# Four-layer diffusion block on one core: the first gate and up tiles of each layer by eight plain block products instead of seven-product sums

## The chip, the core and the metric

The kernel runs on one core of a Trainium2 chip. The metric is the device time of one execution in microseconds (us). TensorE (PE in the rows) multiplies, VectorE (DVE) and ScalarE (ACT) prepare operands and evacuate results, GpSimd (POOL) helps, and SyncE (SP) issues nearly all loads from one in-order queue.

## The reference

Each of four layers is a token mixer (four different ones) followed by a SwiGLU feed-forward block. Only the second half matters here:

```
xs = xs + ms[2] * os_                                   # mixer's residual, through w_o
h  = modulate(rms_norm(xs, norm2_g[li]), ms[3], ms[4])
xs = xs + ms[5] * ((silu(h @ w_gate) * (h @ w_up)) @ w_down)
```

There are 1024 features, 2816 hidden features and 640 tokens (512 latent, 128 context), and each layer also needs its modulation vectors, `silu(cond) @ w_mod`, a 1024 by 6144 matrix.

## The kernel before, in words

Values are split into a rounded high part and a remainder (`hi`, `lo`), and every product is three matmuls: hi·hi, hi·lo, lo·hi. Activations lie features by tokens. The 2816 hidden features are 22 tiles of 128; tile i and tile i + 11 form pair i, and each pair has a gate matrix and an up matrix (`mats`, m = 0 to 21: gate of pair 0, up of pair 0, gate of pair 1, and so on).

For one such matrix the weights A are two by two blocks (tile i or i + 11, by the two halves of 512 features) and the activations B are two by two blocks (feature half, by token halves of 320). `gate_up` takes the four result blocks from seven block products in place of eight: 11·11, 12·21, S2·T2, S1·T1, S3·T3, 22·T4 and S4·22. S1 to S4 are sums of weight blocks that DVE makes (`make_a`), T1 to T4 are sums of activation blocks (`make_b`). A block product is four feature slices of three matmuls, 128x128 weights by 320 tokens. Each weight block or sum is split by a cast on ACT (`whi`) and a subtraction on DVE (`wlo`) in `two`. `Net.slot` hands out the buffers in turn: 4 for loaded blocks (`raw`), 9 each for `whi` and `wlo`, 4 for sums.

The order around the change, in `rest`: the last two output tiles of the w_o projection are computed token half by token half (`halves_first`), so that the RMS norm of the first half (`stat`: squares, a sum over partitions by PE, `rstd`) can go on while PE works on the second half. `make_b` is a generator: its first eight steps make blocks 11 and 21 (first token half), its ninth, in the program of before, makes T1 to T4 and block 22. The generators of the first two matrices are advanced between these steps. `fill` issues pieces of the next layer's modulation product: a burst of 16 small matmuls (32 in the trace) over four 512 KB loads (`rawm`, four buffers), whose buffers can be loaded again only when PE has read them. A scheduler then sets the final order on each engine, so the program's text gives only priorities. In layer 4 there is no next layer and no burst.

`self.sq`, `raws`, `rstd` and the names `hh`/`hl` are the squares, the scaled inputs, the norm's factors and the high and low parts of activation blocks; `big` and `sm` are PSUM tiles, `t` the squares' tile and `x` the residual stream.

Of the kernel before, what the change touches and what calls it, by code (L numbers as in the profile page):

```python
# [8 lines left out]
F32 = mybir.dt.float32  # L9
F32R = mybir.dt.float32r  # L10
# [4 lines left out]
P = 128  # L15
# [4 lines left out]
T = 640  # L20
# [242 lines left out]
class Net:  # L263
# [361 lines left out]
    def make_b(self, pool, L, B, raws):  # L625

        nc = self.nc
        lo, hi = slice(0, 320), slice(320, T)  # L630
        t3 = [pool.tile([P, 2, 320], F32, tag="a", name="raw", bufs=16) for _ in range(HALF // 2)]
        slots = [self.new_act() for _ in range(ND)]
        for tag, w in (("c", T), ("d", 320)):
            slots += [[pool.tile([P, w], F32R, tag=x + tag, name=x, bufs=HALF) for x in ("hh", "hl")] for _ in range(HALF)]
        shift = self.mods[L][0][:, 24:24 + ND]
        more = pool.tile([P, ND + HALF], F32, tag="more", name="more")
        self.sub(nc.vector, more[:, :ND], shift[:, :, 1], shift[:, :, 0])
        self.sub(nc.vector, more[:, ND:], shift[:, HALF:, 0], shift[:, :HALF, 0])

        done = []  # L640

        def two(name, slot, c, x, bias=None):
            h, l = (y[:, c] for y in slots[slot])
            if bias is None:
                nc.scalar.copy(h, x)  # L645
                done.append(self.sub(nc.vector, l, x, h.bitcast(F32)))
            else:
                nc.scalar.activation(h, x, AF.Identity, bias=bias)
                done.append(nc.vector.scalar_tensor_tensor(l, x, bias, h.bitcast(F32), ALU.add, ALU.subtract))  # L649
            B.setdefault(name, []).append((h, l))  # L650

        def raw(d, c):
            with contextlib.ExitStack() as st:
                if len(done) >= 2:
                    st.enter_context(self.tc.issue_after(done[-2].ins))
                nc.vector.tensor_tensor(raws[d][:, c], raws[d][:, c], self.rstd[:, c], ALU.mult)

        for d in range(ND):
            raw(d, lo)
            two(("11", "21")[d // HALF], d, lo, raws[d][:, lo], shift[:, d, 0:1])  # L660
            yield
        for i in range(HALF):
            for d in (i, i + HALF):
                raw(d, hi)
                p, m = raws[d][:, NL:], more[:, d:d + 1]
                nc.scalar.activation(p, p, AF.Identity, bias=m)
            a, b, t = raws[i], raws[i + HALF], t3[i // 2][:, i % 2]
            self.sub(nc.vector, t, b[:, hi], a[:, hi])
            self.sub(nc.vector, a[:, hi], a[:, hi], a[:, lo])
            two("T1", i, hi, a[:, hi])  # L670
        for i in range(HALF):
            a, b, t = raws[i], raws[i + HALF], t3[i // 2][:, i % 2]
            nc.vector.tensor_tensor(a[:, lo], t, a[:, lo], ALU.add)
            two("T2", ND + i, lo, a[:, lo], shift[:, i + HALF, 0:1])
            self.sub(nc.vector, b[:, lo], b[:, lo], a[:, lo])
        for i in range(HALF):
            two("T3", ND + i, hi, t3[i // 2][:, i % 2], more[:, ND + i:ND + i + 1])
        for i in range(HALF):
            two("T4", ND + HALF + i, lo, raws[i + HALF][:, lo])
        for i in range(HALF):  # L680
            two("22", i + HALF, hi, raws[i + HALF][:, hi], shift[:, i + HALF, 0:1])
        yield

    def make_a(self, L, name, i):
# [13 lines left out]
    def block(self, out, A, B, start, stop):  # L698

        h, l = self.two(A, self.nc.vector)  # L700
        for k, (xh, xl) in enumerate(B):
            c = slice(k * P, (k + 1) * P)
            self.mm(out, h[:, c], xh, start and k == 0, False)
            self.mm(out, h[:, c], xl, False, False)
            self.mm(out, l[:, c], xh, False, stop and k == len(B) - 1)

    def gate_up(self, fp, L, name, i, B, pair):

# [28 lines left out]
        self.block(a, A["12"], B["21"], False, True)  # L737
        result(0, 0, a)
        yield
        if i == 0:  # L740
            self.block(d, A["S1"], B["T1"], True, True)
        self.block(b, A["S2"], B["T2"], True, True)
        add(v1, b, s1)
        if i:
            self.block(d, A["S1"], B["T1"], True, True)
        self.block(b, A["S3"], B["T3"], False, True)
        yield
        add(v2, b, s1)
# [3 lines left out]
        self.block(d, A["S4"], B["22"], False, True)  # L752
        result(0, 1, d, v1)
        if up:
            for r in (1, 0):
                hi, lo = (fp.tile([P, T], F32R, tag="a", name=n, bufs=16) for n in ("ah", "al"))
                nc.scalar.copy(hi, pair[r])
                self.sub(nc.vector, lo, pair[r], hi.bitcast(F32))
                pair[r] = (hi, lo)
        yield  # L760


# [36 lines left out]
    def rest(self, L):  # L799

        nc, tc, a = self.nc, self.tc, self.a
        with tc.tile_pool(name=f"ffn{L}", bufs=1, reuse_waits="tile") as fp:
# [24 lines left out]
            def ahead(m):  # L827
                n, i = mats[m]
                gens[m] = self.gate_up(fp, L, n, i, B, pairs[i])
                next(gens[m])  # L830
            ahead(0)
            ahead(1)
            next(gens[0])
            next(gens[1])
            next(B_steps)
            for part, (i0, i1) in enumerate(PAIRS):
                if part:
                    ahead(2 * i0)
                for m in range(2 * i0, 2 * i1):
                    if m > 1:  # L840
                        next(gens[m])
                    next(gens[m])
                    if 0 < m < 2 * i1 - 1:
                        ahead(m + 1)
                    next(gens[m])
                    while done < todo * (m + 1) // len(mats):
                        self.fill(1)
                        done += 1
# [906 lines left out]
```

## Time and profile before

| | us |
|---|---|
| median of 3 runs (lowest, highest) | 3220.17 (3213.5, 3220.33) |
| the profiled execution, its own time | 3216.05 |
| its span in the trace | 3214.0 |
| PE busy with matmuls | 3029.7 (94%) |
| DVE busy | 2161.6 (67%) |
| ACT busy | 1528.5 (48%) |
| mean granted TensorE clock | 0.976 |

The span runs from the first to the last instruction in the trace; the execution's own time has 2.05 us around it. A busy PE is an upper bound, since matmuls overlap. The mean clock says that a small part of the span ran at the lower of TensorE's two levels, 1.2 and 2.4 GHz.

### The profile page before, as it was taken

To read this page: it belongs to the slowest core of one execution; us is meant where nothing else is said; L and a number is where in the kernel's file an instruction comes from. 1 tells how busy PE (TensorE), PEld (TensorE's weight loads), DVE (VectorE), ACT (ScalarE), POOL (GpSimd) and SP (SyncE) were. 2 spreads that over 40 slices of the span, in tenths; PEclk is the share of its full clock that TensorE was granted. 3 is DMA by queue.
4 is the path that set the end of the run, shared out by engine and by line. 5 is a ranking of instruction groups with operands and counts; after the bars stand their busy time and mean duration, and the time that the engine had idled before them with its cause. 6 is when DMAs were issued, how large, how long until landed. Compare 5 with 4: busy or idle time off the path is not lost.

```text
span 3214.0 us, 57273 instructions
## 1 busy us (share of the span) xinstructions
PE 3029.7 (94%) x21901; PEld 2841.6 (88%) x21901; DVE 2161.6 (67%) x4522; ACT 1528.5 (48%) x3264; POOL 607.1 (19%) x691
## 2 busy tenths in 40 slices
PE   7998989999999989999986899899999999899999
PEld 6997879999988779999985778899998878799999
DVE  5555587666586768585768766867575775875765
ACT  4555454333356755242446664434243576543432
POOL 2553200000044420000025542000001553100000
PEclk9998999999999999999998999999999999899999
DMA  8346563232433342222211224522233111132322
GB/s 265 97 123 208 176 224 102 70 92 94 147 102 128 112 155 76 83 83 76 87 53 37 63 75 143 170 89 80 83 132 118 52 32 32 53 99 70 96 66 86
DMA packets 159027, 331.41 MB, mean 103 GB/s; under 512 B 18592, under 2 KB 40480, under 8 KB 158752
## 3 DMA queue, kind: packets, MB, share of 16 engines
q1 hardware_dynamic: 155584, 323.46, 32.3%
q8 instruction: 173, 2.83, 0.4%
q10 hardware_dynamic: 3168, 4.28, 0.4%
q14 instruction: 102, 0.84, 0.1%
HBM read 303.86 MB, written 4.28 MB: 96 GB/s over the span
## 4 chain that ended last, share of the span: by engine, by line
PE 81%; DVE 8%; DMA 5%; ACT 3%; issue 1%; POOL 1%; SPq 0%; DVEq 0%; ACTq 0%; POOLq 0%
PE big L271 53%; PE sm L271 18%; PE S L271 6%; PE tp L1009 3%; DMA rawm<-in_wmod 3%; DMA k<-k 1%; PE tp L271 1%; DMA raw<-in_wall 1%; DVE st L1030 1%; ACT p L1031 1%; DVE x L603 1%; DVE wlo L319 1%; ACT pt L285 0%; DVE qs L958 0%; DVE hl L999 0%
## 5 line engine op out<-in xcount | busy, mean ns | idle before, releaser
L271 PE MATMUL big<-hh,whi 128*128 128x320 f32 x2720 | 825.4, 313 | 11.7 <-ACT hh L645 5.6
L271 PE MATMUL big<-hl,whi 128*128 128x320 f32 x2720 | 829.0, 311 | 6.3 <-DVE hl L649 3.6
L271 PE MATMUL big<-hh,wlo 128*128 128x320 f32 x2720 | 821.0, 310 | 0.0
L318 ACT CAST whi<-raw 128x512 fp32r<-128x512 f32 (+2 forms) x636 | 383.3, 607 | 709.2 <-PE big L271 554.0
L271 PEld LDWEIGHTS big<-hh,whi 128*128 128x128 f32 x2720 | 508.8, 190 | 25.8 <-ACT hh L645 7.8
L271 PEld LDWEIGHTS big<-hl,whi 128*128 128x128 f32 x2720 | 510.1, 189 | 12.0 <-DVE hl L649 6.2
L271 PEld LDWEIGHTS big<-hh,wlo 128*128 128x128 f32 x2720 | 508.2, 189 | 0.1
L319 POOL TENSOR_TENSOR wlo<-raw,whi 128x512 fp32r<-128x512 f32 (+2 forms) x148 | 196.7, 1342 | 1634.0 <-ACT whi L318 1600.6
L319 DVE TENSOR_TENSOR wlo<-raw,whi 128x512 fp32r<-128x512 f32 (+1 forms) x488 | 325.1, 670 | 142.1 <-ACT whi L318 136.1
L318 ACT CAST whi<-sum 128x512 fp32r<-128x512 f32 x352 | 217.6, 619 | 300.1 <-PE big L271 264.6
L271 PE MATMUL big<-ah,wlo 128*128 128x320 f32 x1408 | 329.1, 309 | 0.0
L271 PE MATMUL big<-ah,whi 128*128 128x320 f32 x1408 | 329.0, 310 | 0.0
L271 PE MATMUL big<-al,whi 128*128 128x320 f32 x1408 | 328.6, 309 | 0.0
L319 DVE TENSOR_TENSOR wlo<-sum,whi 128x512 fp32r<-128x512 f32 x352 | 240.8, 684 | 54.5 <-ACT whi L318 52.9
L1041 POOL TENSOR_SCALAR p<-p,st 128x640 f32<-128x640 f32 (+2 forms) x256 | 197.7, 778 | 285.2 <-DVE st L1040 172.0
L603 DVE SCALAR_TENSOR_TENSOR x<-big,mod,x 128x128 f32<-128x128 f32 (+2 forms) x384 | 146.2, 432 | 150.7 <-PE big L271 150.3
L271 PEld LDWEIGHTS big<-ah,whi 128*128 128x128 f32 x1408 | 237.3, 188 | 1.3 <-issue 0.8
L271 PEld LDWEIGHTS big<-al,whi 128*128 128x128 f32 x1408 | 237.3, 188 | 0.3
L271 PEld LDWEIGHTS big<-ah,wlo 128*128 128x128 f32 x1408 | 237.3, 188 | 0.2
L271 PE MATMUL sm<-whi,hh 128*128 128x256 f32 (+1 forms) x770 | 225.1, 297 | 1.7 <-DVE qs L287 1.1
L271 PE MATMUL sm<-wlo,hh 128*128 128x256 f32 (+1 forms) x770 | 223.3, 292 | 0.2 <-POOL wlo L319 0.2
L271 PE MATMUL sm<-whi,hl 128*128 128x256 f32 (+1 forms) x770 | 223.1, 291 | 0.0
(260 smaller groups left out, 5419.3 us busy)
## 6 DMA issues: line engine op xcount, KB each, us to landing
raw<-in_wall SPq DMA_DIRECT2D x676, 256.0 KB, 2.6
rawm<-in_wmod SPq DMA_DIRECT2D x176, 512.0 KB, 5.8
k<-k SPq DMA_DIRECT2D x38, 384.0 KB, 4.2
bias<-in_nabias SPq DMA_DIRECT2D x16, 576.0 KB, 7.2
raw<-in_wmod SPq DMA_DIRECT2D x32, 256.0 KB, 5.7
qpe<-pes SPq DMA_DIRECT2D x56, 80.0 KB, 2.1
raw<-in_wall SPq DMA_DIRECT2D x32, 128.0 KB, 2.1
out_y<-x ACTq DMA_DIRECT2D x8, 320.0 KB, 2.2
```

The costliest lines, as they stand in the source:

```text
L271: return self.nc.tensor.matmul(out, lhsT=lhsT, rhs=rhs, start=start, stop=stop, skip_group_check=True)
L318: self.nc.scalar.copy(hi, raw)
L319: eng.tensor_tensor(lo, raw, hi.bitcast(F32), ALU.subtract)
L603: self.last = self.nc.vector.scalar_tensor_tensor(xs, halves[b][:, p0:p1], self.mcol(L, i, d, c), xs, ALU.mult, ALU.add)
L1009: self.nc.tensor.transpose(out, in_, self.net.ident)
L1030: nc.vector.tensor_reduce(nm, s, axis=AX.XY, op=ALU.max, negate=True)
L1031: nc.scalar.activation(p.rearrange("p (a b) -> p a b", a=2), s, AF.Exp, bias=nm, accum_out=den)
L1041: nc.gpsimd.tensor_scalar(p, p, rd, 1.0, ALU.mult, ALU.mult)
```

## The change

For pair 0 of each layer a new generator `first_pair` replaces the two seven-product generators. It loads the four weight blocks of gate and the four of up, splits each one, and computes the eight result blocks one token half after the other: all four of the first half from B blocks 11 and 21, then all four of the second half from 12 and 22. `make_b` therefore makes block 12 as well (`h12`, new) and 22 early, and T1 to T4 in a step of its own afterwards; they are read first by pair 1. The splitting of the pair's result is moved into `pair_parts`, unchanged, and `gate_up` loses its special case for pair 0.

```
             for d in (i, i + HALF):
                 raw(d, hi)
                 ...
+            x12 = pool.tile([P, 2, 320], F32R, tag="a", name="h12", bufs=16)
+            slots.append([x12[:, j:j + 1].rearrange("p a b -> p (a b)") for j in range(2)])
+            two("12", len(slots) - 1, slice(0, 320), raws[i][:, hi], shift[:, i, 0:1])
+            two("22", i + HALF, hi, raws[i + HALF][:, hi], shift[:, i + HALF, 0:1])
+        yield
+        for i in range(HALF):
             a, b, t = raws[i], raws[i + HALF], t3[i // 2][:, i % 2]
...
-        for i in range(HALF):
-            two("22", i + HALF, hi, raws[i + HALF][:, hi], shift[:, i + HALF, 0:1])
         yield
...
+    def first_pair(self, fp, L, B, pair):
+        nc = self.nc
+        W = {}
+        for name in ("gate", "up"):
+            for r, f in enumerate((0, NF // 2)):
+                for n in range(2):
+                    raw = self.slot("raw")
+                    nc.sync.dma_start(raw, self.a["wall"][WIDX[L, name, f][0] + n])
+                    W[name, r, n] = self.two(raw, nc.vector)
+        pair.extend(fp.tile([P, T], F32, tag="t", name="y", bufs=4) for _ in range(2))
+        for c in range(2):
+            for name in ("gate", "up"):
+                for r in range(2):
+                    out, y = self.ps("big")[:, :320], pair[r][:, 320 * c:320 * c + 320]
+                    for n in range(2):
+                        h, l = W[name, r, n]
+                        for k, (xh, xl) in enumerate(B[f"{n + 1}{c + 1}"]):
+                            w = slice(k * P, (k + 1) * P)
+                            self.mm(out, h[:, w], xh, n == 0 and k == 0, False)
+                            self.mm(out, h[:, w], xl, False, False)
+                            self.mm(out, l[:, w], xh, False, n == 1 and k == HALF - 1)
+                    if name == "gate":
+                        self.silu = nc.scalar.activation(y, out, AF.Silu)
+                    else:
+                        nc.vector.tensor_tensor(y, y, out, ALU.mult)
+            yield
+        self.pair_parts(fp, pair)
+        yield
...
-            ahead(0)
-            ahead(1)
-            next(gens[0])
-            next(gens[1])
+            first = self.first_pair(fp, L, B, pairs[0])
+            next(first)
             next(B_steps)
+            next(first)
+            next(B_steps)
+            next(first)
```

The scheduler's order shows what this moves. First PE in layer 1, where the first products of the feed-forward block begin, before (`whi_5192` is block 11 of gate, `whi_5228` that of up; `hh_5053` and `hh_5055` are the first two slices of B block 11):

```order
L271 MATMUL big_5186<-hh_5053,whi_5192 128x320
L271 MATMUL big_5224<-hh_5053,whi_5228 128x320
L271 MATMUL sm_5742<-consts_78,modev_5740 128x8 x2
L271 MATMUL big_5186<-hl_5054,whi_5192 128x320
L271 MATMUL big_5186<-hh_5053,wlo_5193 128x320
L271 MATMUL big_5186<-hh_5055,whi_5192 128x320
L271 MATMUL big_5224<-hl_5054,whi_5228 128x320
L271 MATMUL big_5224<-hh_5053,wlo_5229 128x320
```

And the same place now (`whi_5172`, `whi_5184`, `whi_5196`, `whi_5208` are the first blocks of gate and up for both tiles):

```order
L271 MATMUL big_5220<-hh_5053,whi_5172 128x320
L271 MATMUL big_5246<-hh_5053,whi_5184 128x320
L271 MATMUL big_5272<-hh_5053,whi_5196 128x320
L271 MATMUL big_5298<-hh_5053,whi_5208 128x320
L271 MATMUL big_5107<-t_5023,consts_78 128x320
L271 MATMUL big_5220<-hl_5054,whi_5172 128x320
L271 MATMUL big_5220<-hh_5053,wlo_5173 128x320
L271 MATMUL big_5246<-hl_5054,whi_5184 128x320
```

Every slice of B now meets four weight blocks in place of two. Next PE where the third burst of the modulation product stands in layer 1, before:

```order
L271 MATMUL big_5224<-hl_5060,whi_5228 128x320
L271 MATMUL big_5224<-hh_5059,wlo_5229 128x320
L271 MATMUL sm_6041<-rawm_5738,cond_61 32x256 x4
L271 MATMUL sm_6041<-rawm_5736,cond_61 32x256 x4
L271 MATMUL sm_6041<-rawm_5734,cond_61 32x256 x4
L271 MATMUL sm_6041<-rawm_5732,cond_61 32x256 x4
L271 MATMUL big_5186<-hh_5061,whi_5245 128x320
```

And now, where `big_5536` to `big_5538` are the sums of gate of pair 1 and `big_5641` is one of up of pair 1:

```order
L271 MATMUL big_5538<-hh_5053,whi_5593 128x320
L271 MATMUL big_5538<-hl_5054,whi_5593 128x320
L271 MATMUL big_5641<-hh_5053,whi_5645 128x320
L271 MATMUL big_5641<-hl_5054,whi_5645 128x320
L271 MATMUL sm_6025<-rawm_5722,cond_61 32x256 x4
L271 MATMUL sm_6025<-rawm_5720,cond_61 32x256 x4
L271 MATMUL sm_6025<-rawm_5718,cond_61 32x256 x4
L271 MATMUL sm_6025<-rawm_5716,cond_61 32x256 x4
L271 MATMUL big_5536<-hh_5061,whi_5559 128x320
```

The third burst has moved from the first quarter of pair 0 into pair 1; 211 matmuls into `big` now stand between it and the second burst (26 before). Last the SP queue of layer 1, from the fifth weight load of pair 0 on; before:

```order
L691 DMA raw_5208<-in_wall 128x512
L691 DMA raw_5212<-in_wall 128x512
L691 DMA raw_5214<-in_wall 128x512
L455 DMA rawm_5162<-in_wmod 128x1024
L455 DMA rawm_5164<-in_wmod 128x1024
```

And now (`raw_5520`, `raw_5522`, `raw_5524` are blocks 21, 22 and 11 of gate of pair 1):

```order
L720 DMA raw_5206<-in_wall 128x512
L720 DMA raw_5212<-in_wall 128x512
L695 DMA raw_5520<-in_wall 128x512
L695 DMA raw_5522<-in_wall 128x512
L695 DMA raw_5524<-in_wall 128x512
L455 DMA rawm_5162<-in_wmod 128x1024
L455 DMA rawm_5164<-in_wmod 128x1024
```

The loads of the second burst (`rawm_5162` and three more) now stand behind three loads of pair 1, each of which waits for a `raw` buffer.

## Rows read from the trace of the kernel before

**Rows 1.** The page: busy time by engine, and its row on weight loads.

```profile
PE 3029.7 (94%) x21901; PEld 2841.6 (88%) x21901; DVE 2161.6 (67%) x4522; ACT 1528.5 (48%) x3264; POOL 607.1 (19%) x691
...
raw<-in_wall SPq DMA_DIRECT2D x676, 256.0 KB, 2.6
```

**Rows 2.** Windows: start of feed-forward in layers 1 to 4, one low-clock stretch, a later pair.

```profile
core 0: us, PE busy (x) PEld busy (x) DVE busy (x) ACT busy (x) POOL busy (x), PEclk, DMA share, GB/s
417.00:470.00 53.00, 44.59 (x348) 37.71 (x349) 46.56 (x105) 30.01 (x65) 0.00 (x0) 0.94 0.68 243
1184.00:1240.00 56.00, 46.81 (x324) 41.47 (x317) 50.29 (x109) 32.48 (x67) 0.00 (x0) 0.91 0.38 127
1993.00:2050.00 57.00, 46.12 (x357) 37.59 (x346) 47.47 (x108) 30.94 (x67) 0.00 (x0) 0.91 0.66 228
2768.00:2816.00 48.00, 37.93 (x220) 35.26 (x219) 46.22 (x99) 31.57 (x64) 0.00 (x0) 0.89 0.19 55
2780.64:2787.47 6.83, 3.98 (x13) 3.64 (x14) 6.58 (x15) 5.34 (x13) 0.00 (x0) 0.50 0.00 0
500.00:525.00 25.00, 25.00 (x173) 25.00 (x172) 22.57 (x40) 12.24 (x22) 0.00 (x0) 1.00 0.27 85
```

**Rows 3.** PE's waits in those four windows, longest first: total us, times, longest.

```profile
PE sm L271 <- DMA rawm<-in_wmod: 7.7, 4, 2.6
...
PE sm L271 <- DMA rawm<-in_wmod: 5.3, 2, 2.7
...
PE sm L271 <- DMA rawm<-in_wmod: 10.1, 4, 4.3
...
PE big L271 <- ACT hh L645: 4.4, 1, 4.4
```

**Rows 4.** The chain that ended last, layer 1: start us, us, what.

```profile
417.03 7.89 DMA rawm<-in_wmod
...
428.42 6.49 DMA rawm<-in_wmod
```

**Rows 5.** Timeline of PE, layer 1: start us, us, what, idle before.

```profile
401.96 0.31 PE L271 MATMUL big<-hh,whi 128*128 128x320 f32 x1
...
405.34 0.31 PE L271 MATMUL big<-hh,wlo 128*128 128x320 f32 x1
...
410.16 0.81 PE L271 MATMUL big<-t,consts 128*128 128x320 f32 x2 [2.65 <-DVE t L496]
...
414.96 1.93 PE L271 MATMUL sm<-rawm,cond 128*32 128x256 f32 x32
...
425.06 3.32 PE L271 MATMUL sm<-rawm,cond 128*32 128x256 f32 x32 [1.44 <-DMA rawm<-in_wmod]
```

**Rows 6.** Timeline of DVE, layer 1.

```profile
403.99 0.68 DVE L319 TENSOR_TENSOR wlo<-sum,whi 128x512 fp32r<-128x512 f32 x1
...
405.74 1.12 DVE L603 SCALAR_TENSOR_TENSOR x<-big,mod,x 128x320 f32<-128x320 f32 x3
...
416.06 0.23 DVE L608 TENSOR_TENSOR more<-mod 128x8 f32<-128x8 f32 x2
...
419.55 0.48 DVE L656 TENSOR_TENSOR raw<-raw,rstd 128x320 f32<-128x320 f32 x1
419.95 0.68 DVE L695 TENSOR_TENSOR sum<-sum,raw 128x512 f32<-128x512 f32 x1
420.55 0.54 DVE L649 SCALAR_TENSOR_TENSOR hl<-raw,mod,hh 128x320 fp32r<-128x320 f32 x1
421.01 0.48 DVE L656 TENSOR_TENSOR raw<-raw,rstd 128x320 f32<-128x320 f32 x1
```

**Rows 7.** Timeline of the SP queue, layer 1: issues.

```profile
406.28 1.76 SPq L455 DMA_DIRECT2D rawm<-in_wmod  x4
...
456.31 13.92 SPq L691 DMA_DIRECT2D raw<-in_wall  x6
```

**Rows 8.** Timeline of ACT, layer 1.

```profile
464.93 0.63 ACT L318 CAST whi<-raw 128x512 fp32r<-128x512 f32 x1 [1.17 <-DMA raw<-in_wall]
```

More of the change, by code (lines that the diff above doesn't have):

```diff
@@ L705, in block, with pair_parts @@
             self.mm(out, l[:, c], xh, False, stop and k == len(B) - 1)
+    def first_pair(self, fp, L, B, pair):
[26 more added lines that the diff above has]
+        yield
+    def pair_parts(self, fp, pair):
+        for r in (1, 0):
+            hi, lo = (fp.tile([P, T], F32R, tag="a", name=n, bufs=16) for n in ("ah", "al"))
+            self.nc.scalar.copy(hi, pair[r])
+            self.sub(self.nc.vector, lo, pair[r], hi.bitcast(F32))
+            pair[r] = (hi, lo)
     def gate_up(self, fp, L, name, i, B, pair):
@@ L739, in gate_up @@
         yield
-        if i == 0:
-            self.block(d, A["S1"], B["T1"], True, True)
         self.block(b, A["S2"], B["T2"], True, True)
         add(v1, b, s1)
-        if i:
-            self.block(d, A["S1"], B["T1"], True, True)
+        self.block(d, A["S1"], B["T1"], True, True)
         self.block(b, A["S3"], B["T3"], False, True)
@@ L754, in gate_up @@
         if up:
[L755 to L759, printed above, removed]
+            self.pair_parts(fp, pair)
         yield
@@ L841, in rest @@
                         next(gens[m])
-                    next(gens[m])
+                        next(gens[m])
                     if 0 < m < 2 * i1 - 1:
                         ahead(m + 1)
-                    next(gens[m])
+                    if m > 1:
+                        next(gens[m])
                     while done < todo * (m + 1) // len(mats):
```

## The prediction

> **What bounds the kernel now.** I read the page first: PE is busy for 94% of the span, the other engines far less [rows 1]. So time can be gained only where PE waits, where its clock is low, or by giving it less to do, and this change gives it more. Next I looked for the waits. A window in a later pair of gate and up has PE busy 25.00 of 25 us at full clock, with DVE at 22.57 [rows 2]: nothing is to be had there, and DVE has only about a tenth to spare. The windows at the start of the four feed-forward blocks differ: PE is busy 44.59 of 53 us, 46.81 of 56, 46.12 of 57 and 37.93 of 48 [rows 2], so it stands idle for 8.41, 9.19, 10.88 and 10.07 us, **38.55 us** together. The granted clock there is 0.94, 0.91, 0.91 and 0.89, where 1.00 is 2.4 GHz and 0.50 is 1.2 GHz. At two levels a mean of 0.94 over 53 us is 6.4 us at the low one; the four windows have 6.4 + 10.1 + 10.3 + 10.6 = 37.4 us of it. In one such stretch, of 6.83 us, PE was busy for 3.98 only [rows 2], so 2.85 us of it are idle time that is counted already; I take the rest as busy. Work at half the clock takes twice as long, so (37.4 - 2.85) / 2 = **17.3 us** are lost to the clock.
>
> Whom PE waits for is in the waits of those windows. In layers 1 to 3 it is above all the bursts: 7.7, 5.3 and 10.1 us, 23.1 together, until a `rawm` load has landed. In layer 4, which has no bursts, it is ACT and DVE with the T blocks, 4.4 us in the longest [rows 3]. The chain explains the bursts: a `rawm` load takes 6.5 to 7.9 us from issue to landing [rows 4], and can be issued only when the burst before has read its buffer. So bursts come about every 10 us at best (425.06 back to 414.96 is 10.1 [rows 5]), and before the change the scheduler put four of them into a stretch in which PE had little else that was ready.
>
> **Added products.** Eight block products in place of seven, for two matrices and 12 matmuls each: 24 more per layer, 96 in all. The 24 rows of w_o's last half run from 401.96 to 405.34 [rows 5], 23 steps of 0.147 us. 96 x 0.147 = **14.1 us** more, all of it on PE, which nothing hides.
>
> The Trainium skill (TensorE: Matmul & The Clock Gate, Back-to-back issue gap) puts the gap of an isolated full-clock matmul at columns / 2.4 + 2.5 ns, here 136 ns. By that figure, as an estimate, the added products would cost 13.0 us and the sum would be 1.1 us lower. The trace has 147 ns, and I go by it.
>
> **Removed from DVE and ACT.** Per layer eight weight sums, six `wlo`, ten additions of results and, against them, four new `hl` for block 12. DVE's steps from start to start are 0.40 us (320 columns, two inputs), 0.60 (512) and 0.46 (`hl`) [rows 6]: 4.8 + 3.6 + 4.0 - 1.8 = 10.6 us less DVE work per layer. ACT loses six casts and two copies and gains four. Neither is counted as a gain; they are the cover for the next step.
>
> **Does PE still wait for B?** The order gives each slice of B to four weight blocks, 12 matmuls or 1.76 us, while DVE makes a slice in 0.40 + 0.46 = 0.86 us, or 1.46 with one step of 512 columns between. So once the first slice is there, PE is the slower one. For the second half I add up DVE's rows in the new order, from `more` (416.06 [rows 6]) to the last slice of block 12: 23 steps of 0.40, 15 of 0.46, two of 0.60 and a few small ones, 18.5 us. PE, starting some 2 us later, needs the last slice of block 12 after 14.3 us for the first half and 3.2 more: 19.5 us. To the last slice of T2 it is 30.8 us for DVE and 38 for PE, to the last of T4 35.2 and 47. DVE keeps ahead by 1 us at the tightest place and then by 7 to 12, although a stall of ACT (it evacuates the first result before it goes on with block 12) may use up that 1 us. So I take the waits for T blocks and block 12 as gone.
>
> **The bursts.** In the order the second and third burst are now 211 matmuls apart, 31 us, against some 10 us for a load; that wait goes. The next two are 54 matmuls apart, 7.9 us plus the burst of 1.93 [rows 5], 9.9 us: about what a load needs, so up to 1 us may stay. All 38.55 us of idle time are thus taken out, and the new waits counted one by one:
>
> - *The sum before the norm.* On DVE, the first sum for pair 1 now stands between the last residuals before `rstd`. It reads `raw_5522`, whose buffer is free when a `wlo` is done that has its like at 403.99 to 404.6; 2.6 us [rows 1] make 407.2, while DVE is there at 406.86 [rows 6]. With a little for semaphores, 0.6 us, and PE waits at that place already (2.65 us for `t` [rows 5]). This holds for layers 1, 3 and 4, and in layer 2 the second burst hides it.
> - *The second burst.* Its loads stand behind `raw_5524` in the SP queue, which needs the `wlo` behind that sum: 407.2 + 0.2 + 0.6 + 0.6 = 408.6, so the bursts' loads go out near 409.0 and not at 406.28 [rows 7], 2.7 us later. The fourth then lands near 416.8, where PE took the burst at 414.96: 1.9 us, the 0.6 above included. Layer 3 is alike; in layer 2 PE reached the place later in any case, and I take nothing.
> - *The first slice* in layer 4: 0.7 us.
>
> New waits ahead of the first product: 1.9 + 0 + 1.9 + (0.6 + 0.7) = **5.1 us**, with ends of 0 and 10 (twice each). The clock: waits of 1.44 us [rows 5] were followed by a low stretch and others of 2.65 were not, so I give back two stretches of half the 6.83 us of [rows 2] each, at half the speed, **3.4 us** of time (ends 0 and 7). For small waits up to pair 1, the burst included, 0.6 per layer, **2.5 us** (ends 0 and 8).
>
> **The sum.** -38.55 - 17.3 + 14.1 + 5.1 + 3.4 + 2.5 = -30.8 us. Made against the profiled execution, 3216.05, this gives 3185.2. That execution lies 4.1 us under the median of the runs; from the median the sum ends at 3189.4. I say 3187. With all new costs at zero it is -41.8, 3174; with all at their upper ends -16.8, 3199 to 3203.
>
> **Rivals.**
>
> *The low clock stays.* The waits that are left, shorter ones, could keep as much time at 1.2 GHz. For it: 1.44 us was enough once. Against: in the later pair, without waits, the clock is 1.00 [rows 2]. Then the 17.3 us are not won, and the 3.4 is within them: -16.9, 3199.
>
> *The T blocks are late in pair 1.* DVE has 2.4 us to spare per pair [rows 2], and 13 us of work on T1 to T4 per layer are now put off. If DVE were stopped on the way, by results that PE has not finished or by late loads, T2 to T4 would be waited for: 5 us per layer, about half of today's idle time, would come back. -30.8 + 20 = -10.8, 3205. Against it is DVE's lead of 7 us and more.
>
> *The bursts move into pairs that need the queue* (slower). The bursts now stand in pairs 1 and 2, and each reload puts 2 MB into SP's queue ahead of weight blocks. The trace shows what that does: a weight load issued at 456.31, right after four burst loads [rows 7], was waited for until 464.93 [rows 8], 8.6 us and not 2.6 [rows 1]. The block 22 of up of pair 1 stands so in the new queue; DVE would stop at its sum, and PE behind it. Eight bursts with 6.0 us each are +48 us: -30.8 + 48 = +17, 3233. It decides from 3.9 us per burst on. By my count the sums from that block are wanted 2.3 us after they would be there, so the lateness is covered, and later pairs without bursts catch up.
>
> The Trainium skill (DMA: Bandwidth & Descriptors, Queues, rings and completion order) says that on each DMA engine descriptors are consumed in the order of the ring. By that rule, a weight load behind a burst must wait for it, and the 8.6 us agree.
>
> *The change does not do what it says*: the bursts' waits stay, since loads and not B set them. Then only the 15.4 us of other idle time and layer 4's 3.7 us of low clock go: -15.4 - 3.7 + 14.1 + 5.1 + 2.5 = +2.6, 3219, no change. The order speaks against it.
>
> **Chances.** Forecast 0.69; low clock 0.12; late T blocks 0.10; queue 0.05; no effect 0.04. A measurement of this kernel can tell about 0.2%, 6.4 us, from no change. The forecast, the clock and the T blocks are faster, which with a small part taken off for mixtures is 0.91; 0.04 the same, 0.05 slower. The forecast and the clock rival hold 0.81 and lie between 3174 and 3203: that is the range.
>
> **What would show it.** Right: in the four windows PE idles for 2 to 4 us each and not 8 to 11; the waits for `rawm` there fall from 23.1 to below 5 us; the clock is 0.97 or more; PE has 96 more matmuls; DVE some 10 us less work per layer. Wrong: PE waiting in pair 1 for `hl` of T blocks or for sums after a late `raw`, or a longer wait for `t` before the norm, with a low clock after it. The forecast fails above all if the waits ahead of the first product are twice what I took and each brings a low stretch.

## The result, and the profile after

The changed kernel took 3174.76 us (median of 4 runs, 3168.55 to 3176.22), the kernel before beside it 3216.84: a ratio of **0.9866**, 95% interval 0.9846 to 0.9886, or 37 to 50 us less. A second set of runs gave 3174.64 against 3221.75, 0.9862 (0.9845 to 0.9878). The forecast, 3187, had the direction and the term that gives most of the gain, pair 0's idle time; 0.9866 of 3216.84 is 3173.7 and lies just under the range. Some 12 us of gain were not foreseen.

The page after, engine line (it answers to [rows 1]); then windows: the stretch around the norm, pair 0 of layers 1 to 4, and the start of pair 1 in layer 1.

```profile
PE 3019.5 (95%) x21997; PEld 2841.6 (90%) x21997; DVE 2115.7 (67%) x4442; ACT 1517.6 (48%) x3248; POOL 610.1 (19%) x691
```

```profile
core 0: us, PE busy (x) PEld busy (x) DVE busy (x) ACT busy (x) POOL busy (x), PEclk, DMA share, GB/s
402.00:417.00 15.00, 13.80 (x124) 10.62 (x123) 12.13 (x27) 8.67 (x20) 5.75 (x5) 1.00 0.64 221
417.00:450.00 33.00, 33.00 (x246) 31.92 (x244) 30.51 (x71) 25.03 (x55) 0.00 (x0) 1.00 0.20 76
450.00:480.00 30.00, 27.80 (x231) 25.18 (x224) 20.26 (x38) 11.31 (x22) 0.00 (x0) 1.00 0.69 234
1161.50:1177.50 16.00, 13.67 (x113) 9.53 (x112) 10.91 (x24) 7.83 (x19) 2.82 (x2) 0.89 0.62 215
1177.50:1210.00 32.50, 32.50 (x238) 31.72 (x240) 29.45 (x69) 24.57 (x54) 0.00 (x0) 1.00 0.18 66
...
1957.50:1973.50 16.00, 13.39 (x112) 9.30 (x112) 11.02 (x24) 8.17 (x19) 3.75 (x4) 0.89 0.62 210
1973.50:2006.00 32.50, 32.50 (x237) 31.65 (x239) 29.62 (x69) 24.55 (x55) 0.00 (x0) 1.00 0.19 68
...
2719.00:2730.00 11.00, 8.68 (x52) 7.59 (x51) 9.24 (x21) 6.70 (x16) 3.36 (x2) 1.00 0.25 74
2730.00:2764.00 34.00, 33.85 (x227) 33.15 (x227) 31.78 (x72) 26.26 (x57) 0.00 (x0) 1.00 0.06 17
```

The windows that hold pair 0 are 32.5 to 34 us long now, at full clock, with PE idle for 0.15 us in all four together; before they were 48 to 57 us long with 38.55 us idle [rows 2]. The lengths are not of the same work, since in layers 1 to 3 those before hold two to four bursts as well; the idle times are what compares. DVE is at 91 to 93% now: it keeps up, with little to spare. What idle time is left lies around the norm and in pairs 1 and 2. Around the norm the kernel before showed this, in the same columns:

```profile
404.00:417.00 13.00, 10.35 (x105) 7.72 (x104) 9.09 (x22) 7.96 (x18) 5.62 (x4) 1.00 0.53 183
1170.00:1184.00 14.00, 12.21 (x115) 10.08 (x117) 10.07 (x24) 8.70 (x19) 5.66 (x4) 1.00 0.46 170
1980.00:1993.00 13.00, 10.34 (x101) 8.20 (x103) 9.11 (x23) 7.17 (x16) 6.32 (x6) 1.00 0.49 176
2752.00:2768.00 16.00, 11.33 (x52) 9.56 (x51) 10.30 (x24) 8.58 (x19) 5.73 (x4) 0.79 0.05 17
```

The idle time (length less PE busy) of these four was 2.65, 1.79, 2.66 and 4.67, together 11.8 us; it is 1.20, 2.33, 2.61 and 2.32 now, 8.5. Whom PE waits for after the change, layers 1, 3 and 4 around the norm and layer 1 in pairs 1 and 2 (total us, times, longest):

```profile
PE big L271 <- DVE more L608: 0.5, 1, 0.5
PE sm L271 <- DMA rawm<-in_wmod: 0.4, 1, 0.4
PE big L271 <- DVE t L496: 0.3, 1, 0.3
...
PE sm L271 <- DMA rawm<-in_wmod: 1.9, 1, 1.9
...
PE big L271 <- DVE t L496: 1.2, 1, 1.2
PE big L271 <- ACT t L494: 1.1, 1, 1.1
...
PE big L271 <- DVE sv L762: 2.2, 2, 1.5
```

The wait for `t` ahead of the norm was 2.65 us in layer 1 [rows 5]; it is 0.3 now, and the burst behind it waits for its loads instead. In pairs 1 and 2 PE idles for 2.2, 0, 1.7 and 1.6 us by layers, 5.5 together.

**The account.** Pair 0: -38.4. Norm: -3.3. Pairs 1 and 2: +5.5. Clock: the 17.3 of the prediction, and 2.6 us more for layer 4's norm, whose window shows 0.79 (6.83 us of it, from 2756.75, are at 1.2 GHz, with PE busy for 5.23 of them); against them the two windows of 16 us at 0.89, 7.0 us at the low level, 3.5 us of time: -16.4. Products +14.1. Together **-38.5 us**. The second profiled run has a span of 3174.6, 39.4 less than before; the first, 3166.8, belongs to the fastest of its runs; of the 7.8 us between the two, 7.1 lie in the mixers (1446.8 and 1453.9 us), which the change does not touch.

The spans can be split to check this sum. I take in each layer the stretch from the last product of w_o's first token half to the end of w_down: before (405.34:878.44, 1174.13:1633.23, 1982.13:2459.34, 2754.47:3209.97), in the first profiled run of the changed kernel (405.47:870.88, 1163.31:1613.16, 1959.08:2426.73, 2721.71:3162.74) and in the second (407.17:875.02, 1169.89:1618.07, 1967.07:2434.31, 2729.25:3170.57). The sums of the four, in this order:

```profile
sum 1864.91, PE 1814.58 PEld 1769.56 DVE 1281.98 ACT 753.75 POOL 21.66; mean PE 453.64 PEld 442.39 DVE 320.50 ACT 188.44 POOL 5.41
sum 1823.94, PE 1809.80 PEld 1771.12 DVE 1239.70 ACT 741.38 POOL 21.08; mean PE 452.45 PEld 442.78 DVE 309.92 ACT 185.34 POOL 5.27
sum 1824.59, PE 1809.97 PEld 1771.31 DVE 1239.04 ACT 741.59 POOL 20.84; mean PE 452.49 PEld 442.83 DVE 309.76 ACT 185.40 POOL 5.21
```

So these feed-forward stretches are 41.0 and 40.3 us shorter. PE idles in them for 50.3 us before and for 14.1 and 14.6 now, which is what the idle terms of the account add up to (-36.2); some 2 us of the gain lie in none of its terms. The rest of the span, the mixers above all, took 6.2 us less in the first run and 0.9 us more in the second.

### The profile page after: what moved, and what is told of

It is laid out like the page before. It is cut to its first block, busy times and chain, and to the rows that moved or that the text cites. A ratio compares the mean times of both kernels' runs of the same rounds, so it can differ in the third digit from the quotient of the medians.

```text
span 3166.8 us, 57330 instructions
## 1 busy us (share of the span) xinstructions
PE 3019.5 (95%) x21997; PEld 2841.6 (90%) x21997; DVE 2115.7 (67%) x4442; ACT 1517.6 (48%) x3248; POOL 610.1 (19%) x691
## 5 line engine op out<-in xcount | busy, mean ns | idle before, releaser
L271 PE MATMUL big<-hh,whi 128*128 128x320 f32 x2688 | 811.7, 311 | 6.8 <-DVE sv L762 3.9
L271 PE MATMUL big<-hl,whi 128*128 128x320 f32 x2688 | 814.3, 309 | 1.9 <-DVE hl L1037 1.8
L271 PE MATMUL big<-hh,wlo 128*128 128x320 f32 x2688 | 805.8, 309 | 0.0
L271 PEld LDWEIGHTS big<-hh,whi 128*128 128x128 f32 x2688 | 498.8, 188 | 18.6 <-issue 6.9
L319 POOL TENSOR_TENSOR wlo<-raw,whi 128x512 fp32r<-128x512 f32 (+2 forms) x148 | 203.6, 1389 | 1601.6 <-ACT whi L318 1570.1
L271 PEld LDWEIGHTS big<-hl,whi 128*128 128x128 f32 x2688 | 500.6, 188 | 3.8 <-DVE hl L1037 2.8
L271 PEld LDWEIGHTS big<-hh,wlo 128*128 128x128 f32 x2688 | 498.4, 188 | 0.6
L318 ACT CAST whi<-sum 128x512 fp32r<-128x512 f32 x320 | 198.1, 620 | 292.8 <-PE big L271 244.5
L319 DVE TENSOR_TENSOR wlo<-sum,whi 128x512 fp32r<-128x512 f32 x320 | 218.3, 685 | 45.0 <-ACT whi L318 43.2
```

Source lines behind the costliest of these rows:

```text
L271: return self.nc.tensor.matmul(out, lhsT=lhsT, rhs=rhs, start=start, stop=stop, skip_group_check=True)
L318: self.nc.scalar.copy(hi, raw)
L319: eng.tensor_tensor(lo, raw, hi.bitcast(F32), ALU.subtract)
```

## Experiments

All ratios are against the kernel before; the changed kernel stands at 0.9866 and 0.9862. Only part of each edit is shown (`...`).

**1. The bursts, with the old products and with the new ones.** In the kernel before, the bursts are held behind the last matmul of pair 0 (`late_bursts`; in its trace only the one ahead of the norm keeps its place, and the second stands at 468.5, right behind pair 0); in the changed one the third and fourth are issued in pair 0 (`early_bursts`).

```
...
-                    while done < todo * (m + 1) // len(mats):
+                    if m == 1:
+                        self.hold = self.end
+                    while m > 2 and done < todo * (m - 2) // (len(mats) - 3):
...
```
```
+                    if c == 0 and (name, r) != ("up", 1):
+                        self.fill(1)
...
```

> The kernel before, with the bursts of the modulation product kept out of pair 0: only their place changes, products and B blocks stay. If the bursts' waits set pair 0 in layers 1 to 3, as the prediction's largest term has it, 23.1 us of idle time and some 10 us of low clock go: about 3184 us, ratio 0.990. If the bursts only stand in gaps in which PE would wait for T blocks and block 22 anyway, each layer idles like layer 4, about 10 us with waits for hh, hl and sv, and the bursts cost their 1.93 us each elsewhere: 3215 to 3230, ratio 1.000 to 1.004.

> The changed kernel, with the third and fourth burst put back into pair 0 (61 matmuls apart, not 211). If the bursts' place is what made the change fast, most of the gain in layers 1 to 3 is lost: 8 us of waits for rawm per layer come back and a low stretch with each, 3174 + 24 + 8 = about 3206. If the plain products on ready B blocks made it fast, a burst is taken when it has landed and costs its 1.93 us here as there: 3174 to 3180.

Measured: 1.0046 (1.0030 to 1.0062), 15 us *slower*, and 0.9837 (0.9819 to 0.9855). Without the bursts PE's waits in pair 0 of layer 1 are those that layer 4 had before:

```profile
PE big L272 <- ACT hh L649: 4.4, 1, 4.4
PE big L272 <- DVE hl L653: 2.8, 4, 1.3
PE big L272 <- ACT hh L652: 1.7, 2, 1.2
PE big L272 <- DVE sv L723: 1.1, 1, 1.1
PE big L272 <- ACT sv L740: 1.1, 1, 1.1
```

The stretches from the first to the last product of pair 0 in layers 1 to 3:

```profile
424.50:468.25 43.75, 32.66 (x185) 29.98 (x184) 42.06 (x91) 28.63 (x59) 0.00 (x0) 0.88 0.17 49
1197.89:1241.10 43.21, 32.59 (x185) 29.09 (x184) 41.05 (x89) 27.86 (x57) 0.00 (x0) 0.92 0.17 50
2013.12:2056.32 43.20, 32.87 (x185) 29.37 (x184) 41.62 (x90) 28.29 (x58) 0.00 (x0) 0.92 0.16 49
```

That is 11.1, 10.6 and 10.3 us of idle time in place of 8.4, 9.2 and 10.9, none of it for `rawm`. So the 23.1 us that the list of waits puts down to the bursts were not caused by them: without them PE waits about as long for blocks that ACT and DVE make, longest for the cast of T1. Nor did the bursts fill those gaps. In the kernel before, the same stretches (417.77:466.76, 1185.68:1232.92, 1994.55:2047.67) take 48.99, 47.24 and 53.12 us, 19.2 us more, and the ten bursts in them take 1.93 us each, 19.3: they cost their own time there. The 15 us are not the price of the move alone. Of the 21.8 us by which the profiled span is longer, 8.9 lie in the feed-forward stretches and the rest outside them. With the new products, bursts in pair 0 cost no idle time: in layer 1 PE is busy for 36.00 of 36 us in pair 0 and for 55.40 of 55.4 in the two pairs behind it.

**2. Weight sums ahead of the norm.** The eight sums of pair 0 made again, all ahead of the norm, for nothing (`sums_back`; in the kernel before, five of the eight stood ahead of it in layers 1 and 4); the kernel before with them held behind it (`sums_held`); the kernel before with them on GpSimd (`before_pool`).

```
...
+            for x, y, op in (((1, 0), (1, 1), ALU.add), ("S", (0, 0), ALU.subtract),
+                             ((0, 0), (1, 0), ALU.subtract), ((0, 1), "S", ALU.subtract)):
+                s = self.slot("sum")
+                nc.vector.tensor_tensor(s, src[x], src[y], op)
+                src["S"] = s
```
```
...
+                if i == 0:
+                    st.enter_context(self.tc.issue_after(self.first_last.ins))
                 nc.vector.tensor_tensor(raw[n], raw[x], raw[y], op)
```
```
-            nc.vector.tensor_tensor(raw[n], raw[x], raw[y], op)
+            (nc.vector if i else nc.gpsimd).tensor_tensor(raw[n], raw[x], raw[y], op)
```

> The changed kernel, with the eight weight sums of pair 0 made as before on DVE ahead of the norm, and used by nothing: 8 x 0.60 us more DVE work per layer and no other step moved. If DVE's backlog of sums made PE wait for t ahead of the norm, these waits come back (0.28, 0.17 and 1.23 us in layers 1, 3 and 4 now; 2.65, 2.66 and 3.58 before): +7 us, with a low stretch or two +10, 3181 to 3184. If the wait was set by ACT's squares or by PE's last w_o products, nothing changes: 3174.

> The kernel before, with the sums of pair 0 held on DVE behind the last residual of the first token half. If the backlog of sums made PE wait for t, these waits fall from 2.65, 2.66 and 3.58 us to 0.3, 0.2 and 1.2 and the low stretch of layer 4's norm goes: -7 to -10 us there. The sums then stand among the slices of B, so pair 0 may wait longer, up to 4 us per layer: 3207 to 3222 in all. If PE or ACT's squares set the wait, it stays near 2.6 us: 3217.

> The kernel before, with the eight weight sums of pair 0 of each layer made by GpSimd, which is idle there, and not by DVE: 4.8 us less DVE work per layer, products, bursts and B order as before. If DVE's work from the end of w_o to pair 0 set the time before the change too, as the 16 us for eight sums put back say of the changed kernel, 10 to 18 us go: 3200 to 3209, with the waits for t near 0.3 us and shorter waits in pair 0. If PE in pair 0 was held by something else, as with the sums held behind the norm, where the waits for t went and the waits for rawm grew to 11 and 13 us, only layer 4 gains: 3214 to 3222. If GpSimd is too slow (1.39 us for such a step, 11 us for eight), S sums are late: above 3222.

Measured: 0.9917 (0.9898 to 0.9937), 1.0027 (1.0014 to 1.0041) and 1.0009 (0.9999 to 1.0018). With the sums put back the wait is there again, in layers 1 to 4:

```profile
PE big L271 <- DVE t L496: 4.0, 1, 4.0
...
PE big L271 <- DVE t L496: 3.5, 1, 3.5
...
PE big L271 <- DVE t L496: 4.1, 1, 4.1
...
PE big L271 <- DVE t L496: 4.4, 1, 4.4
```

16.0 us of it against 1.7 in the changed kernel, and the clock around the norm falls to 0.79, 0.90, 0.83 and 0.84. About 0.0051 of the ratio, 16 us, is more than the 7 to 10 expected, since a wait at this place also brings low stretches. So in the changed kernel sums at this place cost time. The 16 us are not what the change saved by taking its sums away: eight stand ahead of the norm here and the waits for `t` are longer than in the kernel before, 16.0 us against 8.9.

In the kernel before it was worth nothing. With the sums held, no wait for `t` is left in layers 1 and 3, but the same time comes back at the next wait: for `rawm` 12.0 and 13.8 us from the norm to the end of pair 0, where it was 7.7 and 10.1 [rows 3]. On GpSimd they even left the wait for `t` of layer 4 at 4.0 us. There ACT, which makes the squares behind the casts, stood for late weight blocks (before_pool, layer 4, ACT's waits):

```profile
ACT whi L318 <- DMA raw<-in_wall: 11.9, 3, 5.2
ACT t L494 <- DVE x L603: 6.6, 6, 1.6
```

A `raw` buffer is free only when its sums are done, and GpSimd takes some 1.3 us for one. So sums can delay the norm in two ways, by DVE's time and by the buffers; `sums_back` does not tell the two apart. Taking 4.8 us of work off DVE gave no time while pair 0 was held by the T blocks.

**3. Sums added behind the norm** (`sums_behind`), from the high parts of the blocks:

```
...
+                        s = self.slot("sum")
+                        with self.tc.issue_after(self.b12.ins):
+                            nc.vector.tensor_tensor(s, *(W[name, r, n][0].bitcast(F32) for r, n in (x, y)), ALU.add)
```

> The changed kernel with eight sums per layer added on DVE as in the run with the sums put back, but behind block 12 and 22 and not ahead of the norm (made from the high parts, used by nothing). If it is the place that cost 16 us there, PE does not wait for t more than 0.3 us in layers 1 to 3 and the time is within 5 us of the changed kernel, a wait for a burst (two now stand 12 matmuls apart) of up to 4 us per layer set aside: 3168 to 3184. If it is DVE's work as such, 4.8 us per layer come back in pairs 1 and 2, wherever the sums stand: 3185 to 3192.

Measured: 0.9936 (0.9921 to 0.9950), 3199.3, above both forecasts. The norm keeps its short waits, but pairs 1 and 2 wait for 6.4, 5.4 and 5.2 us for `rawm` in layers 1 to 3, and in layer 4, without bursts, 5.3 us for a cast of weights. It is inconclusive as a price of DVE work, because it also puts pair 1's sums later (they share the four buffers) and two bursts next to each other. It suggests that pair 1 has no slack for late weights.

**4. The price of the products** (`fewer`), the second feature half of one result block left out:

```
-                    for n in range(2):
+                    ns = range(1 if r and c else 2)
+                    for n in ns:
```

> The changed kernel with one of the eight block products of gate and of up left out (the second feature half of the last result block), so that the result is not the reference's: 24 matmuls fewer per layer, as many as the change added. If PE is the bound of pair 0 now, all of their price comes back: 96 x 0.147 = 14.1 us, 3174 to about 3160. If PE there waits for B anyway and the added products lie in gaps, it is 0 to 5 us: 3169 to 3174.

Measured: 0.9807 (0.9790 to 0.9823), 3153.53: 18 us under the changed kernel. All of the 14.1 us comes back, and some 4 more. The traces tell where: the feed-forward stretches, cut as above, have 1795.53 us of PE busy against 1809.80, 14.3 less, and 10.9 us idle against 14.1 and 14.6. PE is the bound of pair 0 now. The Trainium skill's gap of an isolated matmul (TensorE: Matmul & The Clock Gate, Back-to-back issue gap) makes 13.0 us by the estimate of the prediction; the 14.3 us here and the 147 ns of the rows stand above it.

**5. A layer without bursts** (`layer4_only`): `PLAIN = (3,)` chooses the new code for layer 4 and the old one for the others (its edit is not shown).

> The change in layer 4 alone, layers 1 to 3 as before; layer 4 has no bursts. If the gain is PE's waits for B and for the norm, layer 4 gives as much as the others: its idle time of 14.7 us goes to 4, its low clock of 17 us to 0, against 3.5 us of products: -12 to -14 us, 3205, ratio 0.996. If a good part of the change's gain comes through the bursts, it gives clearly less than a quarter of the whole: -4 to -7 us, 3210 to 3213, ratio 0.998.

Measured: 0.9954 (0.9938 to 0.9971), 15 us less, a third of the whole gain from the layer that has no burst. Pair 0 of layer 4 in this kernel:

```profile
2765.60:2799.00 33.40, 33.40 (x228) 33.20 (x227) 31.22 (x72) 25.70 (x56) 0.00 (x0) 1.00 0.04 13
```

**6. Order of B, order of the products.** Block 22 behind T1 to T4 in the program's text (`t_first`), and the second weight row's products of the first token half behind those of the first (`by_row`), so that a slice of B meets two weight blocks at first:

```
-            two("22", i + HALF, hi, raws[i + HALF][:, hi], shift[:, i + HALF, 0:1])
-        yield
...
+        for i in range(HALF):
+            two("22", i + HALF, hi, raws[i + HALF][:, hi], shift[:, i + HALF, 0:1])
```
```
-            for name in ("gate", "up"):
-                for r in range(2):
+            for r, name in [(r, name) for r in range(2) for name in ("gate", "up")]:
+                with contextlib.ExitStack() as st:
+                    if r and not c:
+                        st.enter_context(self.tc.issue_after(row.ins))
...
```

> The changed kernel, with block 22 made behind T1 to T4 as before; products and loads stay. If the new order of B is what the plain products live on, PE waits in the second half of pair 0 for DVE, which has 13 us of T1 to T4 to make before 22 and was only 1 to 7 us ahead: 5 to 11 us per layer, with low stretches, 3174 + 20 to 45 = 3194 to 3219. If the eight products alone do it, since they need fewer sums, it stays within 3 us per layer: 3174 to 3186.

> The changed kernel with the first token half's products of the second weight row held behind those of the first: each slice of B meets two weight blocks at first and not four, as before the change, and the same products follow. If PE keeps up with B only because each slice meets four blocks (1.76 us of work, against 0.86 to 1.46 us in which DVE makes a slice), PE waits for hl up to 0.5 us per slice, 2 to 4 us per layer: 3174 + 8 to 16, with a low stretch or two up to 3195. If what counts is that each half of B feeds eight block products, 14 us of work, in whatever order, the waits are under 1 us per layer: 3170 to 3178.

Measured: 0.9849 (0.9830 to 0.9869) and 0.9828 (0.9807 to 0.9849); neither costs anything. In `t_first` PE waits for nobody from the first product of layer 1 to the end of pair 2, and in `by_row` 0.5 us in layer 1 and 1.2 in layer 3, for `rawm`. But `t_first` did not test what its expectation says: the scheduler moved block 22 forward again. On DVE six of the sixteen T slices, and not all, came ahead of its last slice, which was made 13.1 us behind the first slice of block 12 (427.83 and 440.90), against 10.9 in the changed kernel (423.81 and 434.67). So a delay of 2 us is harmless; block 22 wholly behind T1 to T4 stays untested. `by_row` did what it says, and four weight blocks per slice are not needed. (In both, the scheduler also puts one more burst into pair 0.) What both keep is that pair 0 is made of products on plain B blocks: 14 us of PE work on each half of B, where the seven products had 7 us on blocks 11 and 21 and then stood for T1. What went from DVE with the seven products beside the sums, six `wlo` and ten additions per layer, no run separates from this. In layer 4 before, that first wait for a cast of T1 was the 4.4 us of [rows 3], and it is the same 4.4 in `late_bursts` and `before_pool`.

**7. Versions of the changed kernel.** `tuned`: the loads of gate of pair 1 behind the second burst's, its sums behind the norm. `tuned_early`: that, with the bursts of `early_bursts`. `after_pool`: the sums of pairs 1 and 2 on GpSimd. `row_tuned`: `by_row` and `tuned`. `after_again`: the changed kernel as it is.

```
...
+                if i == 1 and name == "gate" and self.burst is not None:
+                    st.enter_context(self.tc.issue_after(self.burst.ins))
                 nc.sync.dma_start(raw[n], self.a["wall"][at[int(n[0]) - 1] + int(n[1]) - 1])
...
+                if i == 1 and name == "gate":
+                    st.enter_context(self.tc.issue_after(self.lead.ins))
                 nc.vector.tensor_tensor(raw[n], raw[x], raw[y], op)
```

> The changed kernel, with the loads of gate of pair 1 put behind those of the second burst in the SP queue, and its sums behind the norm's last residual on DVE. These are the two places of which the prediction expected 5.1 us of new waits. If the load order sets the second burst's wait (0.42, 1.83 and 1.93 us in layers 1 to 3), it falls to about 0, the norm's other waits stay, and one or two low stretches go: 4 us of idle and 2 to 3 of clock, 3174 to about 3167. If the burst is late for its buffer and not for its place in the queue, the waits stay: 3174. If the loads of pair 1 come too late for their sums, PE waits in pair 1 for 1 to 3 us per layer: 3177 to 3186.

> Two edits of runs before together: the loads of gate of pair 1 behind the second burst's, its sums behind the norm, and the third and fourth burst in pair 0. Each alone was 3164 to 3166. If their gains are apart (1.3 us of norm waits per layer by the one, the waits for sv and rawm in pairs 1 and 2 by the other, 1.1 to 2.2 us in layers 1 and 3), about 3161. If both only hit run-to-run differences of the low clock in the mixers, 3164 to 3170, the same as the changed kernel.

> The changed kernel, with the weight sums of pairs 1 and 2 made by GpSimd: 16 x 0.60 us less DVE work per layer behind the norm and in pairs 0 to 2. If DVE is now the engine without slack there, the waits for sv in pairs 1 and 2 (1.5 and 1.7 us in layers 1 and 3, 1.6 in layer 4) go, and with them small gaps: 3166 to 3170. If PE is the only bound, nothing changes: 3173 to 3176. If GpSimd's sums come late for the first blocks of pair 1: 3178 to 3190.

> Two edits of runs before together: the second weight row's products behind the first's, and the loads and sums of pair 1 behind the second burst's loads and the norm. Alone they gave 3163 and 3164. If one acts in pairs 1 and 2 and the other ahead of the norm, about 3158 to 3160; if both take away the same waits, 3163.

> The changed kernel once more, beside the next three on the same chip, since only four runs of it exist and its profiled one is the fastest of them. If the ratio of 0.9866 was right, about 3175; if the first four runs were on the slow side, as the closely related kernels (0.984 and 0.985) suggest, about 3168.

| | us | ratio, 95% interval |
|---|---|---|
| `after_again` | 3174.64 | 0.9862 (0.9845 to 0.9878) |
| `tuned` | 3163.71 | 0.9842 (0.9823 to 0.9861) |
| `tuned_early` | 3164.06 | 0.9831 (0.9814 to 0.9848) |
| `after_pool` | 3170.11 | 0.9855 (0.9841 to 0.9870) |
| `row_tuned` | 3184.67 | 0.9899 (0.9883 to 0.9915) |

In `tuned` the second burst's wait is 1.1, 1.3 and 1.1 us in layers 1 to 3; in the second run of the changed kernel it was 2.0, 1.8 and 1.4, in the first 0.4, 1.8 and 1.9. Its loads were not late for their place in the queue: SP issues them 0.70 us after the first burst begins in `tuned` (409.05 and 409.75 in layer 1) as in the changed kernel. From this issue to the end of PE's wait it takes 8.4 to 8.6 us in `tuned` and 8.1 to 9.6 in the two runs of the changed kernel, where a block of pair 1 is issued just ahead; so the order may cost the transfer some 0.5 us, with one run to show it. The Trainium skill (DMA: Bandwidth & Descriptors, Queues, rings and completion order) has descriptors consumed in the order of the ring; the shorter transfers fit that and do not prove it. `tuned_early` is about 10 us faster than the changed kernel on the same chip, with intervals that touch; its feed-forward stretches, cut as above, take 1815.3 us against 1823.9 and 1824.6, so most of this gain lies where the edits act. `by_row` stands there as well. `after_pool` is not told from the changed kernel. `row_tuned` missed: its parts gained apart and lost together. Its loss lies where neither edit acts, in the mixers. The four mixer windows of `by_row`, then of `row_tuned`:

```profile
0.00:406.90 406.90, 362.35 (x3127) 329.99 (x3128) 214.25 (x539) 205.93 (x500) 154.62 (x182) 0.96 0.57 173
832.70:1164.90 332.20, 314.38 (x2428) 280.05 (x2427) 227.92 (x596) 187.02 (x491) 132.60 (x151) 0.95 0.36 115
1577.70:1956.50 378.80, 330.01 (x2165) 289.38 (x2164) 264.84 (x600) 226.23 (x506) 157.08 (x193) 0.94 0.24 65
2383.00:2715.60 332.60, 315.83 (x2313) 280.63 (x2312) 216.03 (x434) 190.22 (x431) 141.46 (x151) 0.99 0.20 57
```
```profile
0.00:408.20 408.20, 362.86 (x3125) 329.14 (x3126) 213.99 (x539) 205.11 (x500) 153.55 (x182) 0.95 0.56 172
834.30:1173.00 338.70, 316.55 (x2428) 280.22 (x2428) 228.05 (x597) 187.51 (x491) 132.88 (x151) 0.95 0.35 112
1588.60:1974.80 386.20, 331.20 (x2161) 287.75 (x2160) 263.87 (x600) 225.48 (x505) 157.55 (x194) 0.94 0.23 63
2400.50:2734.40 333.90, 316.03 (x2305) 281.04 (x2304) 214.27 (x434) 189.93 (x431) 141.11 (x151) 0.99 0.20 57
```

The windows sum to 1450.5 and 1467.0 us for the same matmuls: 16.5 of the 20.7 us between the two spans. Most of it, 12.4 us, is PE idle. Why the mixers differ by that much stays open, and it means that differences under some 10 us between whole times say little here unless a window shows them.

## Why the prediction came out short

- **Pair 0's idle time goes.** Right in size, -38.4 of -38.55. Wrong in its reason for layers 1 to 3: the chain and the waits name `rawm`, and I took the bursts for the cause. Experiment 1 shows that PE stood there as long without them, for the T blocks above all, so the rival "the change does not do what it says" had no ground at all, and the 211 matmuls between two bursts were not what helped.
- **The new waits ahead of the first product, 5.1 us.** This is the step that failed, at "the sum before the norm": I priced there what the change adds, and of the sums that it removes I wrote "Neither is counted as a gain". I kept PE's wait for `t` as it was and added 0.6 us, and put the first sum of pair 1 at 407.2, behind a `wlo` "that has its like at 403.99". But the old sums of pair 0, which the change removes, were themselves ahead of the norm. DVE before and DVE after, layer 1:

```profile
389.25 0.69 DVE L695 TENSOR_TENSOR sum<-raw 128x512 f32<-128x512 f32 x1 [6.99 <-DMA raw<-in_wall]
...
390.91 0.68 DVE L695 TENSOR_TENSOR sum<-raw 128x512 f32<-128x512 f32 x1
391.51 1.10 DVE L695 TENSOR_TENSOR sum<-sum,raw 128x512 f32<-128x512 f32 x1
...
393.13 0.68 DVE L695 TENSOR_TENSOR sum<-raw,sum 128x512 f32<-128x512 f32 x1
...
409.64 0.47 DVE L496 TENSOR_TENSOR t<-t 128x320 f32<-128x320 f32 x1
```
```profile
404.52 0.69 DVE L699 TENSOR_TENSOR sum<-raw 128x512 f32<-128x512 f32 x1 [0.64 <-DMA raw<-in_wall]
...
407.39 0.48 DVE L496 TENSOR_TENSOR t<-t 128x320 f32<-128x320 f32 x1
```

  Four sums near 390 and a fifth at 407.84 are gone, everything behind them is earlier, the `wlo` that frees the buffer too: the new sum ran at 404.52, and the norm's last `t` at 407.39 in place of 409.64. PE's waits for `t` fell from 8.9 to 1.7 us in the four layers. The stretch gave back 3.3 us (2.5 in the second profiled run) where 5.1 were charged, 8.4 us of the miss. `sums_back` confirms that sums at this place make PE wait for `t`, though not the price. The gain came in layer 4, which has no burst: 4.67 us of idle time became 2.32, and the low stretch there went. In layers 1 to 3 the idle time went from 7.10 to 6.14 us (6.96 in the second run), since PE without its wait for `t` now stands for the second burst.
- **The second burst**, 1.9, 0 and 1.9 us more by the SP queue: 0.4, 0 and 1.9 in the first profiled run, 2.0, 0 and 1.4 in the second. The size is right by luck, the reason wrong. The loads did not go out near 409.0, 2.7 us later, but 0.70 us after the first burst begins, as before (406.28 [rows 7]). First burst before; first burst and loads now:

```profile
405.58 1.94 PE L271 MATMUL sm<-rawm,cond 128*32 128x256 f32 x32
...
405.71 1.93 PE L271 MATMUL sm<-rawm,cond 128*32 128x256 f32 x32
...
406.41 1.75 SPq L455 DMA_DIRECT2D rawm<-in_wmod  x4
```

  In layer 1 PE comes to the second burst sooner, 8.4 us behind the first and not 9.4, because most of the wait for `t` between them is gone, and so meets loads that it used to find landed. They also land later, 8.1 to 9.6 us after their issue in layers 1 to 3 of the two runs, against 7.8 in layer 2 before.
- **DVE and ACT's lighter load, not counted.** It is 45.9 us of DVE work by the two pages, 11.5 per layer, where 10.6 were counted. That it gives nothing in pair 0 fits `before_pool` (no gain from 4.8 us less); ahead of the norm it was wrong.
- **Does PE wait for B?** No, as forecast; but the reason given, four weight blocks to a slice, is not needed (`by_row`).
- **Clock.** Two low stretches back, 3.5 us of time: the forecast had two and 3.4. Not counted was the low stretch at layer 4's norm, 2.6 us.
- **Small waits up to pair 1, 2.5 us.** 0.15 in pair 0 and 5.5 in pairs 1 and 2. A rival shows there in miniature: DVE waits 8.7 us for `raw` in layer 1's pairs 1 and 2, 4.0 at the longest, and PE then for `sv`. This is the rival of the bursts in the queue, at 3.9 us in layers 1 and 3 together and not 48; with the bursts in pair 0 that wait of PE is gone, while DVE still waits 7.8 us for `raw`. Late T blocks PE did not wait for.
- **Products.** 14.1 us, borne out by `fewer`.

With -3.3 for +5.1, 3 us more in pairs 1 and 2 and 2.6 us more of clock, the forecast's -30.8 becomes -38.5, inside the measured interval. The feed-forward stretches measured gave some 2 us more, 41.0 and 40.3; the rest up to the medians, 42 us, is not resolved from the mixers' differences.

## What to carry to other kernels

An engine that waits for a transfer in a stretch where little else is ready might stand there without the transfer too: before taking that wait for the bound, look at the same stretch of a layer that has no such transfer, or move the transfer away and look who is waited for next. Removed work counts where it stood in the in-order queues, not where its result was used: here sums for pair 0 had stood ahead of the norm. Taking 4.8 us of them off gave nothing while another wait lay behind them, and putting 4.8 us back cost 16 us once that wait was gone. And where a scheduler sets the order, an experiment on order has to be read in its trace first: `t_first` left most of the order as it was.

## What was not expected of the hardware

The mixers, with the same instructions, took in the four versions and runs read above from 1447 us (the changed kernel's first profile; its windows have clocks of 0.97, 0.96, 0.95 and 0.99) to 1467 us (`row_tuned`, 0.95, 0.95, 0.94 and 0.99). So an edit in one stage can come with a change of several microseconds in stages that it does not touch; what decides it was not found.
